# Seven block products also in the first feed-forward product of a two-layer decoder, and V and rotation tables in the shared tile pool

## The chip, the cores and the metric

The kernel runs on one NeuronCore of one Trainium2 chip. The metric is the device time of one execution in microseconds (us); less is better. The engines are PE (matmul, with PEld for its weight loads), DVE (VectorE), ACT (ScalarE), POOL (GpSimd) and SP (SyncE, which issues most DMAs).

## The reference, cut to what matters

```python
D_MODEL, SEQ, DEPTH, N_META = 1024, 512, 2, 16
D_FF = 4 * D_MODEL
...
def squared_relu_mlp(h, w1, w2):
    return jnp.square(jax.nn.relu(h @ w1)) @ w2
...
    for l in range(DEPTH):
        mix = hybrid_mixer(h, w_in[l], mla_q_norm[l], mla_kv_norm[l], w_uq[l], w_ukv[l], w_out[l], pos, valid)
        h = layer_norm(DN_ALPHA * h + mix, ln1_g[l], ln1_b[l])
        h = layer_norm(DN_ALPHA * h + squared_relu_mlp(h, w_ff1[l], w_ff2[l]), ln2_g[l], ln2_b[l])
    return h[:, N_PAD + N_META:]
```

All data are float32. `hybrid_mixer` runs eight heads of stick-breaking attention, eight of latent attention (MLA) and four of retention on one projection of `h`, and one output product over all of them. The rotation tables are the cosines and sines of `apply_rope`. Layer 0 works on 528 tokens (512 and 16 meta tokens), layer 1 on the 512 that are returned.

## The kernel before, in words

**Layout.** Activations lie transposed: 128 features on the partitions, tokens along the columns, so `h` is 8 tiles (`KT`) of up to 528 columns. Each float32 operand is held as two parts of type fp32r, hi (a rounded copy) and lo (the rest); a product of two tiles is three matmuls, hi*hi, hi*lo and lo*hi. `wload` brings 512 columns of weights by a DMA from SP into a tile of pool R; `wsplit` makes hi by a copy on ACT and lo by a subtraction on DVE, both in pool W. Pool U holds 63 tiles of 528 columns for everything else, V has its own pool VC, and five rotation tables lie in constants for the whole run (`tables`, line 520). Eight PSUM banks hold the products; `PM` and `PA` are two streams of the same eight.

**Feed-forward part** (`layer`, from line 1366). D_FF is cut in four quarters `qd` of 8 tiles. `ff1(qd, mt, c0, c1)` makes one tile of relu(h@w1)^2: 24 matmuls (8 tiles of `h`, three each) for a group of columns. In layer 0 the groups are 256 and 272 columns, in layer 1 one of 512. For quarters 0 to 2 the second product is made by `strassen(qd, m)`: for each pair of output tiles the 2 by 2 block product (block rows are the two output tiles, block columns the halves of H = 264 or 256 tokens, the inner blocks tiles i and i+4 of the quarter) is made with seven block products, 12 matmuls of H columns each, in place of eight, in the form of Winograd. `strassen_weights` makes the sums of weights (two by a DMA that adds, issued by POOL, two on DVE), `strassen_inputs` the sums of activations. Quarter 3 is made by plain `ff2`. Between the first product of a quarter and its seven-product part stands tile 0 of the next quarter's `ff1`. `nf=4`: the last four tiles of quarter 3 are made in two halves of columns, so that the layer norm of the first half runs beside the second.

**Order.** A recorder notes every operation (they all carry the profile's line 416), and `schedule` plays them through with the costs in nanoseconds of `_cost`: each engine takes the operation that can start first, then the one of lower rank. Tiles of a pool are handed out in the order in which they were recorded, within its capacity (`fits`); an operation whose tile isn't free waits. The order that comes out is what the engines run.

Of the kernel before, what the change touches and what calls it, by code (L numbers as in the profile page):

```python
# [15 lines left out]
P = 128  # L16
D = 1024
KT = D // P
# [21 lines left out]
    pvo=(-0.2, 0.0), mix=(0.9, 0.0), wl=0.0, wd=0.0, nw=4, nf=4, head=3, wc=512, wa=512,  # L40
# [185 lines left out]
class Recorder:  # L226
# [51 lines left out]
    @staticmethod  # L278
    def _cost(op, ins, outs):
        psum = any(v.t.cls.name == "ps" for v in ins)  # L280
        n = int(np.prod(outs[0].shape[1:])) if outs else 1
        op.ldw = 0.0
        if op.eng == "tensor":
            if op.fn == "transpose":
                n = op.args[1].shape[0]
                op.cost, op.ldw = n * 2 / 2.4 + 2, op.args[1].shape[1] / 1.2
            else:
                lt = op.kw["lhsT"]
                op.cost = n / 2.4 * (4 if lt.dtype == F32 else 1) + 2.5
                op.ldw = lt.shape[1] / (2.4 if lt.dtype == BF16 else 1.2)  # L290
        elif "dma" in op.fn:
            op.cost = 60.0
        elif op.eng == "scalar":
            op.cost = (54 if psum else 94) + 0.833 * n + 93 * (len(ins) - 1) + 93 * (len(outs) - 1)
        elif op.eng == "vector":
            fast = not psum and op.fn in ("tensor_copy", "tensor_scalar", "memset")
            if op.fn in ("bn_stats", "reduce_max"):
                n = int(np.prod(ins[0].shape[1:]))
            op.cost = 62 + n * (0.53 if fast else 1.05) + 62 * sum(isinstance(op.kw.get(k), View) for k in ("scalar", "scalar1", "scalar2"))
        else:  # L300
            op.cost = 80 + n * (2.4 if op.fn in ("tensor_sub", "tensor_add") else 1.2)
# [126 lines left out]
class Builder:  # L428
    def __init__(self, ctx, tc, a):
# [93 lines left out]
    def tables(self):  # L523
# [8 lines left out]
        for n in ("tqe", "tqo", "tkr", "rc", "rs"):  # L532
            tt = self.const(n, [P, NT], F32)
            nc.sync.dma_start(tt, a[n])
            self.tab[n] = tt
# [24 lines left out]
    def strassen_weights(self, l, qd, m):  # L560


        nc, src = self.nc, self.a["wf2"][l, qd, m]
        a11, a12, a21, a22 = (src[:, i:i + 512] for i in range(0, 2048, 512))
        t = {}
        with nc.rank(nc.cur + PR['wd']):
            for name, first, more in (("a12", a12, ()), ("s1", a21, (a22,)), ("a11", a11, ()), ("s3", a21, (a11,)),
                                      ("a22", a22, ())):
                t[name] = self.R.tile([P, 512], F32)
                nc.sync.dma_start(t[name], first)  # L570
                for x in more:
                    nc.gpsimd.dma_start(t[name], x, accum_op=ALU.add)
        w = {}
        for name in ("a12", "a11", "s1", "s2", "s4", "s3", "a22"):
            if name in ("s2", "s4"):
                x, y = ("s1", "a11") if name == "s2" else ("s2", "a12")
                t[name] = self.R.tile([P, 512], F32)
                nc.vector.tensor_add(t[name], t[x], t[y])
            w[name] = self.wsplit(t[name])
        return w  # L580

    def strassen_inputs(self, x, e, eh, el):

        nc = self.nc
        a, b = x
        H = e.shape[1]
        t = self.unit()
        b11, b12, b21, b22 = a[:, :H], a[:, H:2 * H], b[:, :H], b[:, H:2 * H]
        t3, t4, t2, t1 = t[:, :H], t[:, H:2 * H], e, b12
# [3 lines left out]
        nc.vector.scalar_tensor_tensor(out=t4, in0=t2, scalar=-1.0, in1=b21, op0=ALU.mult, op1=ALU.subtract)  # L593
        d = {}
        for x, names in ((b, ("b21", "b22")), (a, ("b11", "t1")), (e, ("t2",)), (t, ("t3", "t4"))):
            n = H * len(names)
            hi, lo = (eh, el) if x is e else (self.unit(F32R)[:, :n], self.unit(F32R)[:, :n])
            self.split(hi, lo, x[:, :n], "a")
            for i, k in enumerate(names):
                d[k] = (hi[:, i * H:i * H + H], lo[:, i * H:i * H + H])  # L600
        return d

# [53 lines left out]
    def ln_back(self, xns, gset, h, c0, c1):  # L656
# [4 lines left out]
        for kt in range(KT):  # L661
# [4 lines left out]
            hf = self.unit()[:, :c1 - c0]  # L666
# [19 lines left out]
    def ln_group(self, r, gset, h, c0, c1, final):  # L686
# [15 lines left out]
        if not final:  # L702
            self.ln_back(xns, gset, h, c0, c1)


    def v_tokens(self, w, b0, rhs, heads):
# [9 lines left out]
        V = self.VC.tile([P, 5, heads, 2, P // heads], F32R)  # L716
# [5 lines left out]
        s0 = p0[:, :P].reshape(heads, P // heads)  # L722
        nc.scalar.copy(V[:, 0, :, 0, :], s0)
        nc.vector.tensor_sub(V[:, 0, :, 1, :], s0, f32(V[:, 0, :, 0, :]))
        s1 = pv.reshape(4, heads, P // heads)
        nc.scalar.copy(V[:, 1:5, :, 0, :], s1)
        nc.vector.tensor_sub(V[:, 1:5, :, 1, :], s1, f32(V[:, 1:5, :, 0, :]))
# [3 lines left out]
    def pv_pair(self, s, hd, V, regs, meta):  # L731
# [5 lines left out]
        for i, j in enumerate(order):  # L737
            v = V[:, j, hd].reshape(P)
# [259 lines left out]
    def ret_attn(self, l, hd, st, V, gate):  # L998
# [73 lines left out]
    def mla_c(self, l, h):  # L1072
# [45 lines left out]
        wkr = self.wload(self.a["win"][l, 29])  # L1118
        kt, kth, ktl = self.unit(), self.unit(F32R), self.unit(F32R)
        krh, krl = self.unit(F32R), self.unit(F32R)  # L1120
        for (c0, c1) in self.groups(True):
# [3 lines left out]
            nc.vector.tensor_mul(kt[:, c0:c1], ps[:, :n], self.tab["tkr"][:, c0:c1])  # L1125
# [8 lines left out]
    def mla_proj(self, l, p, cn, kr):  # L1134
# [19 lines left out]
        for hd in range(2):  # L1154
            tab = self.tab["tqe" if hd == 0 else "tqo"]
# [139 lines left out]
    def layer(self, l, h, first):  # L1295
# [20 lines left out]
        for hd in range(4):  # L1316
# [49 lines left out]
        r_mix, r = r, [None] * KT  # L1366
        nf = PR['nf']
        NQ = NT if full else NX
        H = NQ // 2
        us, ws3 = [[] for _ in range(4)], [{} for _ in range(4)]  # L1370
        raw = [{} for _ in range(4)]
        half = [None]

        def ff1(qd, mt, c0, c1):
            n = c1 - c0
            if mt not in ws3[qd]:
                ws3[qd][mt] = self.wload(self.a["wff1"][l, 8 * qd + mt])
                if qd == 3:
                    us[qd].append((self.unit(F32R), self.unit(F32R)))
                else:  # L1380
                    raw[qd][mt] = self.unit()
            ps = self.mmb()
            self.proj(ps[:, :n], ws3[qd][mt], 0, h, c0, c1)
            rl = self.unit()[:, :n]
            nc.scalar.activation(rl, ps[:, :n], AF.Relu)
            if qd == 3:
                nc.scalar.activation(rl, rl, AF.Square)
                self.split(us[qd][mt][0][:, c0:c1], us[qd][mt][1][:, c0:c1], rl, "a")
                return
            x = raw[qd][mt]  # L1390
            nc.scalar.activation(x[:, c0:c1], rl, AF.Square)
            if c1 == NQ and mt >= 4:
                i = mt - 4
                if i % 2 == 0:
                    half[0] = self.unit(F32R), self.unit(F32R)
                c = slice((i % 2) * H, (i % 2) * H + H)
                us[qd].append(self.strassen_inputs((raw[qd][i], x), self.unit()[:, :H], half[0][0][:, c], half[0][1][:, c]))

        def ff2(qd, mt, w, c0, c1):
            n = c1 - c0  # L1400
            ps = self.mmb()
            self.proj(ps[:, :n], w, 0, us[qd], c0, c1)
            self.accum(ps[:, :n], r[mt][:, c0:c1], None, c0, c1)

        def strassen(qd, m):
            w = self.strassen_weights(l, qd, m)
            if qd == 0:
                for mt in (2 * m, 2 * m + 1):
                    r[mt] = self.unit()
            X, Y, Z = (self.mmb()[:, :H] for _ in range(3))  # L1410
            touched = set()

            def prod(ps, wk, uk, first, last):
                wh, wl = w[wk]
                for i in range(4):
                    b = slice(i * P, i * P + P)
                    uh, ul = us[qd][i][uk]
                    self.mm(ps, wh[:, b], uh, first and i == 0, False)
                    self.mm(ps, wh[:, b], ul, False, False)
                    self.mm(ps, wl[:, b], uh, False, last and i == 3)  # L1420

            def add(ps, row, col, op=ALU.add):
                mt, c = 2 * m + row, slice(col * H, col * H + H)
                o = r[mt][:, c]
                if qd == 0 and (row, col) not in touched:
                    touched.add((row, col))
# [224 lines left out]
```

## Time and profile before

| | |
|---|---|
| median of 3 runs | 1570.37 us (1570.01 to 1570.98) |
| the profiled execution | 1570.71 us, span 1568.9 us |
| mean granted TensorE clock | 0.996 |
| PE, PEld busy | 1535.4 us (98%), 1448.0 us (92%) |
| DVE, ACT busy | 1169.5 us (75%), 880.4 us (56%) |

The span runs from the first to the last instruction; 1.8 us of the profiled execution lie outside it. Busy times are unions of the recorded intervals; a matmul's interval is longer than its share of the engine, since matmuls are pipelined and their ends modelled, so in what follows matmuls are counted per stretch of time.

### The profile page before, as it was taken

Reading aid. Unit: us, or ns where it says so; the run is one execution under the profiler, and the core shown is the slowest. Engines: PE = TensorE matmul, PEld = TensorE weight load, DVE = VectorE, ACT = ScalarE, POOL = GpSimd, SP = SyncE. Lnnn points to the kernel's source line nnn. Section 1 sums busy time; section 2 is a strip of 40 time slices with the busy share of each in tenths; the row PEclk is TensorE's granted clock in tenths of the full one; section 3 lists DMA queues with packets and bytes.
Section 4 is the critical chain, followed back from the end, with each engine's and each line's share of the span. In section 5 each row is a group of like instructions: output and inputs, shape, how many; then the busy total and the mean of one; then the engine's idle time right before and its main releaser. Section 6 shows DMA issues by size and latency. Waiting matters only on the chain.

```text
span 1568.9 us, 30040 instructions
## 1 busy us (share of the span) xinstructions
PE 1535.4 (98%) x11130; PEld 1448.0 (92%) x11130; DVE 1169.5 (75%) x2791; ACT 880.4 (56%) x1979; POOL 145.9 (9%) x249
## 2 busy tenths in 40 slices
PE   6999999999999999999999999999999999999996
PEld 6999999989999999999999999888889898989986
DVE  7778877899787868674467878779997786767635
ACT  5575744578566464645336666445884645555440
POOL 4112100100001000010002112001100010101000
PEclk9999999999999999999999999999999999999998
DMA  6423422322024636354214233423222354545422
GB/s 231 120 70 112 134 68 69 92 65 76 29 84 111 169 101 167 101 147 132 89 61 129 80 96 95 125 68 98 72 68 63 106 150 127 148 135 130 153 61 81
DMA packets 88978, 165.26 MB, mean 105 GB/s; under 512 B 12032, under 2 KB 13312, under 8 KB 88832
## 3 DMA queue, kind: packets, MB, share of 16 engines
q1 hardware_dynamic: 76800, 136.77, 28.2%
q0 software_dynamic: 12032, 26.59, 8.4%
q8 instruction: 87, 1.43, 0.4%
q14 instruction: 59, 0.48, 0.1%
HBM read 142.92 MB, written 2.10 MB: 92 GB/s over the span
## 4 chain that ended last, share of the span: by engine, by line
PE 92%; DVE 4%; ACT 2%; issue 1%; DMA 0%; SPq 0%; DVEq 0%; ACTq 0%; POOLq 0%
PE ps L416 92%; DVE u L416 2%; ACT u L416 2%; DVE t L416 2%; DVE w L416 0%; DMA r<-in_win 0%; SPq L416 0%; DMA u<-u 0%; ACT w L416 0%; ACT t L416 0%; DVE v L416 0%; DVEq L1646 0%; ACTq L416 0%; DVEq L416 0%; POOLq L416 0%
## 5 line engine op out<-in xcount | busy, mean ns | idle before, releaser
L416 PE MATMUL ps<-u,w 128*128 128x256 f32 (+3 forms) x9024 | 1312.6, 303 | 3.1 <-DVE u L416 2.0
L416 PEld LDWEIGHTS ps<-u,w 128*128 128x128 f32 x9024 | 1203.1, 189 | 63.2 <-DVE u L416 3.4
L416 ACT CAST w<-r 128x512 fp32r<-128x512 f32 (+1 forms) x520 | 315.4, 618 | 384.2 <-PE ps L416 352.4
L416 DVE TENSOR_TENSOR w<-r,w 128x512 fp32r<-128x512 f32 (+1 forms) x514 | 350.3, 688 | 179.2 <-ACT w L416 152.4
L416 DVE TENSOR_TENSOR u<-u,u 128x512 fp32r<-128x512 f32 (+11 forms) x467 | 247.1, 552 | 40.2 <-ACT u L416 37.5
L416 ACT ACTIVATE u<-ps 128x256 f32<-128x256 f32 (+7 forms) x237 | 114.1, 486 | 116.6 <-PE ps L416 106.9
L416 ACT CAST u<-u 128x512 fp32r<-128x512 f32 (+6 forms) x247 | 128.8, 540 | 45.9 <-DVE u L416 39.9
L416 DVE TENSOR_TENSOR u<-u,ps 128x256 f32<-128x256 f32 (+3 forms) x220 | 95.4, 436 | 65.0 <-PE ps L416 62.5
L416 DVE TENSOR_TENSOR u<-ps,u 128x16 fp32r<-128x16 f32 (+14 forms) x312 | 115.3, 400 | 21.8 <-ACT u L416 14.6
L416 ACT ACTIVATE u<-u 128x256 f32<-128x256 f32 (+5 forms) x245 | 124.0, 521 | 5.4 <-DVE u L416 1.3
L416 PE MATMUL ps<-ident,u 128*128 128x128 f32 x672 | 104.6, 279 | 15.6 <-DVE t L416 9.6
L416 POOL DMA_DIRECT2D u<-u x112 | 58.2, 525 | 520.8 <-ACT u L416 484.0
L416 PE MATMUL ps<-u,u 128*128 128x512 f32 (+4 forms) x528 | 103.4, 314 | 0.0
L416 PEld LDWEIGHTS ps<-ident,u 128*128 128x128 f32 x672 | 79.8, 142 | 23.8 <-DVE t L416 8.4
L416 POOL DMA_DIRECT2D r<-in_wf x48 | 42.1, 877 | 588.9 <-DVE w L416 255.8
L416 PE MATMUL ps<-u,v 128*128 128x400 f32 (+4 forms) x484 | 89.1, 301 | 2.0 <-DVE u L416 0.6
L416 PEld LDWEIGHTS ps<-u,u 128*128 128x128 f32 x528 | 79.8, 190 | 2.6
L416 PEld LDWEIGHTS ps<-u,v 128*128 128x128 f32 x484 | 72.1, 189 | 7.0 <-ACT u L416 2.5
L416 ACT COPY u<-ps 128x256 f32<-128x256 f32 (+5 forms) x108 | 43.9, 416 | 41.2 <-PE ps L416 39.9
L416 DVE SCALAR_TENSOR_TENSOR u<-ps,u 128x432 f32<-128x432 f32 (+7 forms) x73 | 41.4, 579 | 27.6 <-ACT u L416 24.9
L416 ACT CAST u<-ps 128x16 fp32r<-128x16 f32 (+7 forms) x188 | 49.9, 331 | 18.7 <-PE ps L416 13.3
L416 ACT ACTIVATE u<-ps,t 128x512 f32<-128x512 f32 (+4 forms) x86 | 48.1, 562 | 18.4 <-DVE t L416 16.1
(66 smaller groups left out, 758.1 us busy)
## 6 DMA issues: line engine op xcount, KB each, us to landing
r<-in_wff SPq DMA_DIRECT2D x160, 256.0 KB, 2.9
r<-in_win SPq DMA_DIRECT2D x120, 256.0 KB, 2.9
r<-in_wf SPq DMA_DIRECT2D x120, 256.0 KB, 3.1
r<-in_wout SPq DMA_DIRECT2D x48, 256.0 KB, 2.9
r<-in_wf POOLq DMA_DIRECT2D x48, 256.0 KB, 4.7
u<-u POOLq DMA_DIRECT2D x80, 132.0 KB, 3.6
u<-u SPq DMA_DIRECT2D x48, 66.0 KB, 2.7
u<-in_xm SPq DMA_DIRECT2D x10, 256.0 KB, 5.3
```

Source lines behind the costliest of these rows:

```text
L416: o.ins = getattr(getattr(nc, o.eng), o.fn)(*[r(x) for x in o.args], **{k: r(x) for k, x in o.kw.items()})
```

## The change

The first product gets pairs of tiles (i, i+4) by seven block products too: all pairs of quarters 1 to 3 and pair 3 of quarter 0 (`npl=3` pairs stay plain), 13 of 16. The sums of `h` are made once for each layer. Two of the four pairs of quarter 3's second product are made by seven block products, in place of none. One function `strassen` runs both. In `ff1_pair` the blocks of the output come out of PSUM one after the other, bank X is read after each of x1, x2, x3 and x4, and the squares and the second product's sums are made per block. The residual's start value is a float32 copy of `h` (`raw`) that the layer norm leaves, in place of hi and lo. V (three tiles in place of one of VC) and the rotation tables (loaded in each layer, where they are used) come from pool U, which has 75 tiles. The planner's costs are changed, and the tile of the next quarter between the two products is gone.

```diff
-    pvo=(-0.2, 0.0), mix=(0.9, 0.0), wl=0.0, wd=0.0, nw=4, nf=4, head=3, wc=512, wa=512,
+    pvo=(-0.2, 0.0), mix=(0.9, 0.0), wl=0.0, wd=0.0, nw=4, nf=4, npl=3, head=3, wc=512, wa=512,
...
-                op.cost = n / 2.4 * (4 if lt.dtype == F32 else 1) + 2.5
+                op.cost = 4 + 0.4445 * n
...
-            op.cost = (54 if psum else 94) + 0.833 * n + 93 * (len(ins) - 1) + 93 * (len(outs) - 1)
+            op.cost = (100 if psum else 125) + 0.833 * n + 100 * (len(ins) - 1) + 180 * (len(outs) - 1)
...
-            op.cost = 62 + n * (0.53 if fast else 1.05) + 62 * sum(isinstance(op.kw.get(k), View) for k in ("scalar", "scalar1", "scalar2"))
+            op.cost = 85 + n * (0.55 if fast else 1.04) + 55 * sum(isinstance(op.kw.get(k), View) for k in ("scalar", "scalar1", "scalar2"))
...
-        self.U = Pool(self.sb, "u", NT, 63).stream(63)
+        self.U = Pool(self.sb, "u", NT, 75).stream(75)
-        self.VC = Pool(self.sb, "v", 1280, 3).stream(3)
...
+    def table(self, n):
+        t = self.unit()
+        self.nc.sync.dma_start(t, self.a[n])
+        return t
...
+        load("s1", a21, a22)
+        load("a11", a11)
+        load("a12", a12)
+        w["s1"] = self.wsplit(t["s1"])
+        w["a11"] = self.wsplit(t["a11"])
+        add("s2", "s1", "a11")
+        load("s3", a21, a11)
+        add("s4", "s2", "a12")
+        w["s4"] = self.wsplit(t["s4"])
+        w["s2"] = self.wsplit(t["s2"])
+        load("a22", a22)
+        w["a12"] = self.wsplit(t["a12"])
+        w["s3"] = self.wsplit(t["s3"])
+        w["a22"] = self.wsplit(t["a22"])
...
+    def strassen(self, w, us, order, H, done):
+        X, Y, Z = (self.mmb()[:, :H] for _ in range(3))
+        prods = dict(y=(Y, "a12", "b21", True, True), x1=(X, "a11", "b11", True, False), z1=(Z, "s1", "t1", True, False),
+                     x2=(X, "s2", "t2", False, False), z2=(Z, "s4", "b22", False, True), x3=(X, "s3", "t3", False, False),
+                     x4=(X, "a22", "t4", False, True))
+        n = len(us)
+        for k in order:
+            ps, wk, uk, first, last = prods[k]
...
+                self.mm(ps, wh[:, b], uh, first and i == 0, False)
+                self.mm(ps, wh[:, b], ul, False, False)
+                self.mm(ps, wl[:, b], uh, False, last and i == n - 1)
+            if k in done:
+                done[k](X, Y, Z)
...
+        def ff1_pair(qd, i):
+            w = self.strassen_weights(self.a["wff1"][l, 8 * qd + i], self.a["wff1"][l, 8 * qd + i + 4])
...
+            def square(x, scale, src):
+                nc.scalar.activation(x, src, AF.Relu, scale=scale)
+                nc.scalar.activation(x, x, AF.Square)
...
+            def x1(X, Y, Z):
+                nc.vector.tensor_add(b11, X, b11)
+                square(b11, 1.0, b11)
+            def x2(X, Y, Z):
+                nc.vector.tensor_add(b12, X, b12)
+                square(b12, 1.0, b12)
+                sub(t1, b11, b12)
...
+                    parts(p, ("b11", "t1"))
+            def x3(X, Y, Z):
+                nc.vector.tensor_add(b22, X, z1)
+                square(b22, -1.0, b22)
+                sub(t3, b22, b12)
+                stt(out=t2, in0=t3, scalar=-1.0, in1=b11, op0=ALU.mult, op1=ALU.subtract)
+                parts(t2, ("t2",), *(x[:, o] for x in self.half[0]))
+                if qd < 3:
+                    parts(q, ("b22", "t3"))
+            def x4(X, Y, Z):
+                square(b21, -1.0, X)
+                stt(out=t4, in0=t2, scalar=-1.0, in1=b21, op0=ALU.mult, op1=ALU.subtract)
...
+            self.strassen(w, hs, ("z1", "y", "x1", "z2", "x2", "x3", "x4"), H, dict(
+                z1=lambda X, Y, Z: nc.scalar.copy(z1, Z), y=lambda X, Y, Z: nc.scalar.copy(b11, Y),
+                z2=lambda X, Y, Z: nc.scalar.copy(b12, Z), x1=x1, x2=x2, x3=x3, x4=x4))
...
+            self.strassen(w, us[qd], ("z1", "x1", "z2", "x2", "y", "x3", "x4"), H, dict(
...
-            if qd < 3:
-                for g in gl:
-                    ff1(qd + 1, 0, *g)
...
+        for i in range(npl, 4):
+            ff1_pair(0, i)
+        for m in range(4):
+            ff2_pair(0, m)
+        for qd in range(1, 4):
+            for i in range(4):
+                ff1_pair(qd, i)
+            for m in range(4 if qd < 3 else 4 - nf // 2):
+                ff2_pair(qd, m)
```

## Rows read from the trace of the kernel before

**Rows 1.** The page's part 1: busy us (share of the span) xinstructions.

```profile
PE 1535.4 (98%) x11130; PEld 1448.0 (92%) x11130; DVE 1169.5 (75%) x2791; ACT 880.4 (56%) x1979; POOL 145.9 (9%) x249
```

**Rows 2.** The page's part 4, the chain that ended last, by engine.

```profile
PE 92%; DVE 4%; ACT 2%; issue 1%; DMA 0%; SPq 0%; DVEq 0%; ACTq 0%; POOLq 0%
```

**Rows 3.** Who waited for whom, PE's waits: us in total, times, longest.

```profile
PE ps L416 <- DVE t L416: 10.2, 4, 8.4
PE ps L416 <- DVE u L416: 6.8, 8, 2.3
PE ps L416 <- ACT u L416: 3.8, 5, 1.4
```

**Rows 4.** Busy us (xinstructions) by stretch; then granted clock, DMA share, GB/s.

```profile
core 0: us, PE busy (x) PEld busy (x) DVE busy (x) ACT busy (x) POOL busy (x), PEclk, DMA share, GB/s
300.00:400.00 100.00, 95.82 (x717) 88.81 (x716) 91.21 (x316) 76.58 (x245) 11.24 (x32) 0.98 0.26 74
...
460.00:500.00 40.00, 40.00 (x329) 40.00 (x328) 28.14 (x55) 27.12 (x61) 3.57 (x4) 1.00 0.45 113
...
510.00:540.00 30.00, 30.00 (x248) 30.00 (x247) 27.39 (x58) 12.29 (x21) 2.62 (x3) 1.00 0.69 183
550.00:580.00 30.00, 30.00 (x249) 30.00 (x248) 19.05 (x36) 19.17 (x42) 2.63 (x3) 1.00 0.37 92
595.00:625.00 30.00, 30.00 (x249) 30.00 (x248) 24.28 (x46) 12.66 (x21) 3.50 (x4) 1.00 0.67 178
...
1080.00:1180.00 100.00, 98.64 (x607) 84.88 (x606) 92.34 (x293) 81.11 (x247) 6.60 (x17) 1.00 0.26 76
...
1310.00:1340.00 30.00, 30.00 (x131) 24.36 (x130) 18.82 (x35) 17.79 (x32) 2.62 (x3) 1.00 0.39 102
...
1352.00:1382.00 30.00, 30.00 (x257) 30.00 (x256) 25.39 (x47) 13.54 (x22) 3.50 (x4) 1.00 0.71 190
```

**Rows 5.** Timeline: start us, us of the merged run, engine, operation, count.

```profile
419.89 1.08 DVE L416 TENSOR_TENSOR u<-u,ps 128x256 f32<-128x256 f32 x3 [1.21 <-PE ps L416]
421.67 0.42 DVE L416 TENSOR_TENSOR u<-u,ps 128x256 f32<-128x256 f32 x1 [0.70 <-PE ps L416]
...
602.22 1.14 ACT L416 CAST w<-r 128x512 fp32r<-128x512 f32 x2 [0.83 <-PE ps L416]
...
605.60 1.29 DVE L416 TENSOR_TENSOR w<-r,w 128x512 fp32r<-128x512 f32 x2
```

**Rows 6.** Instruction groups by shape, 450 to 800 us: count | busy us, mean ns.

```profile
L416 DVE TENSOR_TENSOR w<-r,w 128x512 fp32r<-128x512 f32 x159 | 108.5, 690 | 71.2 <-ACT w L416 56.4 <-PE ps L416 8.6 <-issue 0.5
L416 ACT CAST w<-r 128x512 fp32r<-128x512 f32 x160 | 97.0, 620 | 131.5 <-PE ps L416 116.1 <-issue 6.6 <-DVE r L416 4.3
L416 DVE TENSOR_TENSOR u<-u,ps 128x264 f32<-128x264 f32 x68 | 28.9, 427 | 11.0 <-PE ps L416 10.8
L416 DVE TENSOR_TENSOR u<-u,u 128x528 fp32r<-128x528 f32 x36 | 25.3, 702 | 0.0
...
L416 DVE TENSOR_TENSOR r<-r,r 128x512 f32<-128x512 f32 x24 | 16.4, 685 | 0.1
L416 ACT ACTIVATE u<-u 128x272 f32<-128x272 f32 x32 | 13.8, 432 | 0.9
...
L416 ACT ACTIVATE u<-ps 128x272 f32<-128x272 f32 x32 | 12.6, 394 | 3.1 <-PE ps L416 3.0
```

**Rows 7.** DMA issues: count, KB each, median us from issue to landing.

```profile
r<-in_wf SPq DMA_DIRECT2D x120, 256.0 KB, 3.1
r<-in_wf POOLq DMA_DIRECT2D x48, 256.0 KB, 4.7
...
rc<-in_rc SPq DMA_DIRECT2D x1, 264.0 KB, 4.3
```

**Rows 8.** Waits of the queue on SP: us in total, times, longest.

```profile
SPq L416 <- DVE w L416: 969.4, 328, 17.1
```

More of the change, by code (lines that the diff above doesn't have):

```diff
@@ L558, in wsplit, with strassen_weights, load @@
         return hi, lo
-    def strassen_weights(self, l, qd, m):
-        nc, src = self.nc, self.a["wf2"][l, qd, m]
-        a11, a12, a21, a22 = (src[:, i:i + 512] for i in range(0, 2048, 512))
+    def strassen_weights(self, src1, src2):
+        nc = self.nc
+        a11, a12, a21, a22 = src1[:, 0:512], src1[:, 512:1024], src2[:, 0:512], src2[:, 512:1024]
         t = {}
[L566 to L569, printed above, removed]
+        def load(name, first, more=None):
+            t[name] = self.R.tile([P, 512], F32)
+            with nc.rank(nc.cur + PR['wd']):
@@ L570, in strassen_weights @@
                 nc.sync.dma_start(t[name], first)
-                for x in more:
-                    nc.gpsimd.dma_start(t[name], x, accum_op=ALU.add)
-        w = {}
[L574 to L579, printed above, removed]
+                if more is not None:
+                    nc.gpsimd.dma_start(t[name], more, accum_op=ALU.add)
@@ new lines, in add @@
+        def add(name, x, y):
+            t[name] = self.R.tile([P, 512], F32)
+            nc.vector.tensor_add(t[name], t[x], t[y])
+        w = {}
+        load("s1", a21, a22)
[9 more added lines that the diff above has]
+        load("a22", a22)
@@ L601, in strassen_inputs, with parts, run @@
-        return d
+    def parts(self, d, H):
+        def run(x, names, hi=None, lo=None):
+            n = H * len(names)
+            if hi is None:
+                hi, lo = self.unit(F32R)[:, :n], self.unit(F32R)[:, :n]
+            self.split(hi, lo, x[:, :n], "a")
+            for j, k in enumerate(names):
+                d[k] = (hi[:, j * H:j * H + H], lo[:, j * H:j * H + H])
+            return hi, lo
+        return run
+    def strassen_inputs(self, a, b, H, i):
+        t, e = self.unit(), self.unit()[:, :H]
+        if i % 2 == 0:
+            self.half = [(self.unit(F32R), self.unit(F32R))]
+        o = slice((i % 2) * H, (i % 2) * H + H)
+        self.strassen_sums(a, b, a[:, H:2 * H], e, t)
+        d = {}
+        parts = self.parts(d, H)
+        parts(a, ("b11", "t1"))
+        parts(e, ("t2",), *(x[:, o] for x in self.half[0]))
+        parts(b, ("b21", "b22"))
+        parts(t, ("t3", "t4"))
+        return d
@@ L715, in v_tokens @@
                 yield
-        V = self.VC.tile([P, 5, heads, 2, P // heads], F32R)
+        n = 2 * P
+        U = [self.unit(F32R) for _ in range(3)]
+        V = [U[0][:, :n].reshape(heads, 2, P // heads)]
+        for u in U[1:]:
+            V += [u[:, i * n:i * n + n].reshape(heads, 2, P // heads) for i in range(2)]
         p0 = self.mmb()
@@ L1372, in layer, with ff1 @@
-        half = [None]
-        def ff1(qd, mt, c0, c1):
+        us, xs, hs = [[] for _ in range(4)], {}, []
+        touched = set()
+        nf = PR['nf']
+        def ff1(mt, c0, c1):
             n = c1 - c0
[L1376 to L1381, printed above, removed]
+            if mt not in xs:
+                xs[mt] = self.wload(self.a["wff1"][l, mt]), self.unit()
+            w, x = xs[mt]
@@ L1382, in ff1 @@
             ps = self.mmb()
[L1383 removed]
+            self.proj(ps[:, :n], w, 0, h, c0, c1)
             rl = self.unit()[:, :n]
             nc.scalar.activation(rl, ps[:, :n], AF.Relu)
[L1386 to L1391 removed]
@@ L1400, in ff2 @@
+        def ff2(mt, w, c0, c1):
             n = c1 - c0
             ps = self.mmb()
[L1402 removed]
+            self.proj(ps[:, :n], w, 0, plain, c0, c1)
             self.accum(ps[:, :n], r[mt][:, c0:c1], None, c0, c1)
[L1405 to L1426, printed above, removed]
[L1427 to L1445 removed]
@@ new lines, in layer @@
+        for (hi, lo), x in sums:
+            self.split(hi, lo, x, "a")
+        for i in range(npl):
+            us[0].append(self.strassen_inputs(xs[i][1][:, :NQ], xs[i + 4][1][:, :NQ], H, i))
+        for i in range(npl, 4):
[3 more added lines that the diff above has]
+        for qd in range(1, 4):
+            for i in range(4):
+                ff1_pair(qd, i)
+            for m in range(4 if qd < 3 else 4 - nf // 2):
+                ff2_pair(qd, m)
@@ L1471, in layer @@
+        plain = [u["plain"][0] for u in us[3]] + [u["plain"][1] for u in us[3]]
         final = l == DEPTH - 1
-        ws = {mt: self.wload(self.a["wff2"][l, 0, mt]) for mt in range(8 - nf, 8)}
+        ws = {mt: self.wload(self.a["wff2"][l, 3, mt]) for mt in range(8 - nf, 8)}
         for i, g in enumerate(gs):
```

198 lines of the change are left out of this document (102 added, 96 removed).

## The prediction, as it was put on record before the run

> **What bounds the kernel now.** I read the page's busy shares first: PE is busy for 98% of the span, DVE for 75%, ACT for 56% [rows 1]. The chain that ended last says the same, 92% of it is PE [rows 2], and PE's own waits add up to 10.2 + 6.8 + 3.8 = 20.8 us, 8.4 of it in one wait for a tile t of statistics [rows 3]. A busy PE may still be a slow one, so next I counted matmuls per stretch. In the feed-forward part they follow one another without holes: 248 records touch 510:540, two of them lap in from the edges, so one of 264 columns takes 30/246 = 0.122 us; the plain stretch 550:580 gives the same, layer 1's 257 of 256 columns give 30/255 = 0.1176 us, and its 131 of 512 columns 30/129 = 0.2325 us [rows 4]. The reader should see two more things there. In the seven-product stretches DVE is at 27.39 of 30 us (91%, quarter 0) and 24.28 (81%), and PE keeps its full count beside it. And in the latent attention, where DVE shows 91.21 and 92.34 of 100 us and ACT 76.58 and 81.11, the matmul counts drop (717 small and large ones in 100 us): there DVE, ACT and PE hold each other up [rows 4]. So PE's count is what the feed-forward part costs, as long as DVE is not filled.
>
> **The change, part by part.**
>
> *Removed from PE.* A pair of tiles by eight block products is 96 matmuls of H columns, by seven 84. Per layer 13 pairs of the first product and 2 of the second change, 15 in all. Layer 0: 12 x 0.122 = 1.464 us a pair, 22.0 us. Layer 1: plain is 48 of 512 columns, 48 x 0.2325 = 11.16 us; seven products of 256 columns are 84 x 0.1176 = 9.88 us; 1.28 a pair, 19.2 us. Sum 41.2 us; that is the ceiling, since no operation is added to PE.
>
> *Added to DVE in a first-product pair.* Records of DVE overlap: a lone subtraction of 512 columns shows 690 ns [rows 6], but two in a row take 1.29 us, so the second costs 1.29 - 0.69 = 0.60; three of 256 columns take 1.08 us and a lone one 0.42, so (1.08 - 0.42)/2 = 0.33 each, and I take 0.34 for 264 and 0.62 for 528. On ACT two of 512 take 1.14 us, 0.52 each [rows 5]. A pair then needs on DVE 7 weight subtractions and 2 weight sums (9 x 0.60), 3 adds from PSUM and 4 sums (7 x 0.34), and the lo parts of 528, 528, 528 and 264 columns (3 x 0.62 + 0.34): 9.98 us, beside 84 x 0.122 = 10.25 us of PE. Plain it was 4 x 0.60 + 4 x 0.34 + 2.20 = 5.96. In layer 1 it is 9.84 beside 9.88. In quarter 3 one more short subtraction makes it 10.32. ACT: 7 x 0.52 for the weights, 3 copies and 8 squares or relus at about 0.3 to 0.43 [rows 6], 2.0 for the splits, some 9.4 us. So DVE goes from half full to 97 to 101% full, and ACT to about 90%.
>
> [...]
>
> *What that costs.* Below: nothing. Averaged over a quarter DVE needs 4 x 9.98 and, with 9 x 0.60 + 7 x 0.34 = 7.78 for each pair of the second product, 4 x 7.78, together 71.0 us in 8 x 10.25 = 82.0 (87%), and pool W holds one pair's weights (14 tiles) ahead; at 91% by the record, in 510:540, PE lost nothing [rows 4]. Above: each pair by itself, with DVE kept only 92% busy as in 1080:1180 [rows 4]. Layer 0: 9.98/0.92 = 10.85, 0.60 over PE, x13 = 7.8; layer 1: 9.84/0.92 = 10.70, 0.82 over, x13 = 10.7; quarter 3's extra 0.34/0.92 x 8 = 3.0; 21.5 us. I take 12, a bit over half: the stretch is nearer to the seven-product one in its kind of work, but at its demand no row shows PE undisturbed, and each of the eight passages from first to second product must drain DVE's chain (add, relu, square, subtraction, split) with no tile of the next quarter between.
>
> *Start of the part.* The sums of `h` are new: 4 x (4 x 0.34 + 0.62 + 2 x 0.34) = 10.6 us of DVE per layer, after the second half's layer norm. Of the nine tiles that stood before the first seven-product part, 329/48 = 6.9 were made after 460 us [rows 4]; with three tiles fewer, PE has four left there (4 x 48 x 0.122 = 23.4 us) and one new pair, 33.7 us; DVE has 8 x 0.60 for weights, 10.6, the inputs of three pairs 3 x 3.56 = 10.7, the pair's 9.98 and 5.4 for the next weights: 41.5. Above, 7.8 us a layer; below about 1, since five of those seven splits and the late inputs can come while PE is at the first products. Before, DVE had 28.14 of these 40 us filled [rows 4]. I take 2.5, for two layers 5.
>
> *Second product.* Residual from `raw`: one instruction for each block in place of two, 16 x 0.34 = 5.4 us of DVE less in quarter 0, hidden as now; nothing.
>
> *DMAs.* A new pair takes 5 loads by SP and 2 adding ones by POOL, in place of 4 and 0; adding ones go from 48 to 108, 4.7 us to landing, behind 3.1 for the load they add to [rows 7]. The DMA share stands at 0.69 in a seven-product stretch [rows 4] and a pair lasts 10 us, so I take nothing; a cover lost shows as POOL waiting and PE waiting for weights, about 2 us at a passage, which the 12 holds.
>
> *Tables and V.* Ten table loads in place of five, each 4.3 us to landing [rows 7], in SP's queue behind weight loads, which wait for tiles up to 17.1 us [rows 8]; behind a late one stands one DVE multiplication and the projection's bank. Below nothing, above 4.3 us a layer for one late table; I take nothing, since the pool hands tiles out ahead. V's copies in three pieces, not two, add 24 short pairs, 24 x (2 x 0.33 - 0.60) = 1.4 us on DVE; nothing.
>
> *Planner's costs.* A matmul of 264 columns is planned at 121 ns (112 before), as measured; a DVE subtraction of 512 at 617 (600) and an ACT copy at 551 (520), 3 to 6% over the rows [rows 5]. The mixer is put in another order; sign unknown, zero, and 5 us either way, a quarter of PE's 20.8 us of waits [rows 3].
>
> *Sum.* 1570.7 (the profiled execution, 0.3 over the median) - 41.2 + 12 + 5 = 1546.5; against the median 1546.
>
> **The rivals.**
>
> *DVE becomes the bound.* Both upper bounds: 1570.7 - 41.2 + 21.5 + 15.6 = 1566.6, with a late table in each layer 1575; around 1568. For it: 97 to 101% demand; the latent attention, where 92% goes with lost matmuls. Against it: the 87% over a quarter.
>
> *DVE's records do not overlap in the new mix.* Dependent instructions (sum on sum) follow one another without the gain of 0.69 - 0.60 = 0.09 us. If all paid the whole record [rows 6], a pair would need 9 x 0.690 + 7 x 0.427 + 3 x 0.702 + 0.427 = 11.7 us, 1.5 over PE, in layer 1 (0.69 and 0.42) 11.6, 1.75 over, x13 each = 42: 1570.7 - 41.2 + 42 + 5 = 1577. Against it: pairs in a row in rows 5 do overlap. [...]
>
> *Bank X is the bound* (slower). x2, x3 and x4 follow one another into one bank, and each must wait until DVE has read the last: a read of 0.43 us behind an instruction of 0.60 in DVE's queue, 1.0 each, two a pair. If PE has nothing to put between, 26 x 2.0 = 52 us: 1570.7 - 41.2 + 52 + 5 = 1586. It decides from (41.2 - 5)/26 = 1.39 us a pair. Behind x3 then stand x4 and the next pair's products; only the next pair's z1 and y can fill, if two triples of banks and its weights are free. For it: DVE's queue is full now. Against it: the second product ends with x3, x4 in the same way, and its stretches keep full count [rows 4].
>
> *All is hidden.* 1570.7 - 41.2, with 2 to 8 us for the starts: 1532 to 1538.
>
> That the products are not saved can't be: their number is fixed.
>
> **How the numbers follow.** Forecast, 1546 (1538 to 1560): 0.53. DVE the bound, 1560 to 1575: 0.19. No overlap: 0.02. Bank X: 0.10. All hidden: 0.16. The range 1532 to 1571 holds all of the first, nearly all of the last and most of the second, 0.83. A measurement tells about 0.2% (3 us): faster takes the first and last and 0.10 of the second, 0.79; within 0.2%, 0.07 of it; slower the rest, 0.14.
>
> **What would show it.** Layer 0 must lose 15 x 12 = 180 matmuls; in layer 1 15 x 48 = 720 of 512 columns become 15 x 84 = 1260 of 256. In the new first-product stretches DVE should show 93% or more, beside about 245 matmuls in 30 us; under 235, DVE is the bound, and the waits of PE name DVE u. Waits of PE before x3 and x4 inside the pairs, not at the ends of quarters, would be bank X. In quarter 0, where DVE has 41.5 us of work in 33.7 of PE, PE should wait a few us for hi and lo parts. Wrong would be a mixer that moves by more than 5 us, or new waits of PE for DMA r.

## The result and the profile after

The changed kernel takes 1547.31 us, the median of four runs (1544.35 to 1547.67), against 1570.19 (1569.96 to 1570.98) for the kernel before, run beside it: a ratio of 0.9851, 95% interval 0.9839 to 0.9862. The forecast was 1546, faster. The profiled execution took 1546.99 us, with a span of 1545.2.

The page's parts 1 and 4 of the changed kernel, which answer to [rows 1] and [rows 2]:

```profile
PE 1504.6 (97%) x11490; PEld 1443.6 (93%) x11490; DVE 1303.8 (84%) x3131; ACT 963.7 (62%) x2263; POOL 197.9 (13%) x309
...
PE 87%; DVE 9%; ACT 2%; issue 1%; DMA 0%; SPq 0%; DVEq 0%; ACTq 0%
```

PE has 360 records more, as it must: 180 fewer in layer 0, and in layer 1 1260 of 256 columns in place of 720 of 512. Its busy time falls by 30.8 us, while DVE's rises by 134.3 and ACT's by 83.3. DVE's share of the chain that ended last goes from 4 to 9%.

PE's waits (in total, times, longest), to be read against [rows 3]:

```profile
PE ps L414 <- DVE u L414: 10.9, 16, 2.0
PE ps L414 <- DVE t L414: 9.2, 2, 7.9
PE ps L414 <- ACT w L414: 5.2, 9, 1.5
PE ps L414 <- ACT u L414: 2.5, 5, 0.6
```

One kind of wait is new: PE waits for a weight tile w from ACT, nine times. No wait for a DMA is among them.

Busy time by stretch, with the columns of [rows 4]. The first row and the one of 1060:1160 are the latent attention; 545:575 and 1295:1325 lie in the new first-product stretches; the rest is quarter 0 and the passages from the first to the second product:

```profile
300.00:400.00 100.00, 96.57 (x731) 89.51 (x730) 92.05 (x322) 77.62 (x250) 11.24 (x32) 1.00 0.26 74
478.00:498.00 20.00, 16.88 (x134) 16.25 (x133) 19.61 (x41) 15.59 (x36) 2.86 (x4) 1.00 0.55 148
500.00:530.00 30.00, 30.00 (x249) 30.00 (x248) 26.96 (x53) 12.60 (x22) 5.25 (x6) 1.00 0.74 186
545.00:575.00 30.00, 30.00 (x249) 30.00 (x248) 29.08 (x57) 26.45 (x64) 4.38 (x5) 1.00 0.69 171
575.00:587.00 12.00, 10.45 (x68) 9.72 (x68) 10.22 (x21) 6.74 (x16) 1.75 (x2) 0.86 0.40 112
660.00:670.00 10.00, 8.45 (x67) 8.02 (x66) 9.59 (x20) 6.81 (x15) 0.88 (x1) 1.00 0.55 140
1060.00:1160.00 100.00, 99.74 (x610) 85.69 (x610) 91.04 (x290) 80.16 (x245) 7.79 (x21) 1.00 0.26 74
1230.00:1250.00 20.00, 17.43 (x129) 16.62 (x128) 18.04 (x38) 14.10 (x31) 3.47 (x4) 0.91 0.61 160
1295.00:1325.00 30.00, 30.00 (x257) 30.00 (x256) 28.95 (x59) 27.23 (x67) 4.38 (x5) 1.00 0.69 174
1324.00:1331.00 7.00, 6.34 (x48) 5.60 (x47) 7.00 (x16) 4.84 (x12) 1.75 (x2) 1.00 0.67 171
```

Inside the new stretches DVE is busy for 97% (29.08 and 28.95 of 30 us) and ACT for 88 to 91%, and PE keeps its full count: 249 records of 264 columns and 257 of 256, as in [rows 4]. What PE loses lies at the passages. In 575:587, 98 matmuls of 0.122 us would fit and 68 stand there: 30 x 0.122 = 3.7 us gone. In 660:670 it is 15 of 82 (1.8 us), in 478:498, quarter 0, 30 of 164 (3.7 us).

The whole account, from the starts of all matmuls (what each start comes later than the count of its width allows): the products save 40.1 us; PE loses 20.9 in the two feed-forward parts, 9.0 of it in quarter 0 (3.9 and 5.1) and 11.9 at the later passages (4.0 and 2.1 at the first two of layer 0, 0.6 to 2.1 at the others); the rest comes out 4.5 us shorter. 1570.7 - 40.1 + 20.9 - 4.5 = 1547.0.

The passage at 575:587 by itself, PE's timeline (start, us, count, and in brackets its idle time before and who ended it):

```profile
575.80 3.68 PE L414 MATMUL ps<-u,w 128*128 128x264 f32 x29
580.00 0.51 PE L414 MATMUL ps<-u,w 128*128 128x264 f32 x2 [0.52 <-ACT w L414]
581.14 0.51 PE L414 MATMUL ps<-u,w 128*128 128x264 f32 x2 [0.64 <-ACT w L414]
582.05 3.29 PE L414 MATMUL ps<-u,w 128*128 128x264 f32 x13 [0.40 <-ACT u L414]
```

and ACT's:

```profile
579.33 0.61 ACT L414 CAST w<-r 128x512 fp32r<-128x512 f32 x1
579.84 0.41 ACT L414 CAST u<-u 128x264 fp32r<-128x264 f32 x1
580.16 0.42 ACT L414 ACTIVATE u<-u 128x264 f32<-128x264 f32 x1
580.48 0.60 ACT L414 CAST w<-r 128x512 fp32r<-128x512 f32 x1
```

PE runs two matmuls and stops, twice: each time 0.05 to 0.06 us after ACT has made a hi copy of a weight (579.33 + 0.61 = 579.94, PE at 580.00). Matched with the order in which the program issues them, these are the first products, z1 and x1, of the *second* pair of the second product. The two tiles of pool w that ACT writes for them had been released only at 578.62, by x4 of the last first-product pair, and at 578.99, by z1 of the first pair of the second product; ACT, which has other work in its queue without a gap there, came to them 0.7 and 1.5 us later. So what is late is a weight tile, because pool w's 14 tiles are one pair's seven hi and seven lo parts. The third pause, 0.40 us before 582.05, is another: there PE waits for an input, the last pair's, which has come through DVE and ACT. After these pauses the granted clock falls to 0.50 for 3.4 us:

```profile
582.30:585.70 3.40, 3.40 (x16) 3.38 (x16) 2.08 (x4) 0.22 (x1) 0.31 (x1) 0.50 0.51 172
```

so that the mean of the row 575:587 is 0.86. Some 1.7 of this passage's 4.0 us are that (an estimate: half of 3.40 us; by the count, 16 records stand there where 28 would fit, 12 x 0.122 = 1.5).

### The profile page after: what moved, and what is told of

Same layout as the page of the kernel before. It is cut to its first block, busy times and chain, and to the rows that moved or that the text cites. A ratio compares the mean times of both kernels' runs of the same rounds, so it can differ in the third digit from the quotient of the medians.

```text
span 1545.2 us, 31629 instructions
## 1 busy us (share of the span) xinstructions
PE 1504.6 (97%) x11490; PEld 1443.6 (93%) x11490; DVE 1303.8 (84%) x3131; ACT 963.7 (62%) x2263; POOL 197.9 (13%) x309
## 4 chain that ended last, share of the span: by engine, by line
PE 87%; DVE 9%; ACT 2%; issue 1%; DMA 0%; SPq 0%; DVEq 0%; ACTq 0%
PE ps L414 87%; DVE u L414 6%; ACT u L414 2%; DVE t L414 2%; DVE w L414 1%; DMA u<-in_xm 0%; SPq L414 0%; DVE r L414 0%; ACT w L414 0%; DVEq L1738 0%; ACT t L414 0%; DVEq L414 0%; ACTq L414 0%
## 5 line engine op out<-in xcount | busy, mean ns | idle before, releaser
L414 ACT CAST w<-r 128x512 fp32r<-128x512 f32 x610 | 364.5, 617 | 293.0 <-PE ps L414 249.2
L414 DVE TENSOR_TENSOR w<-r,w 128x512 fp32r<-128x512 f32 x604 | 404.8, 686 | 59.2 <-ACT w L414 42.9
L414 DVE TENSOR_TENSOR u<-u,u 128x512 fp32r<-128x512 f32 (+10 forms) x541 | 283.3, 548 | 10.8 <-ACT u L414 8.9
L414 DVE TENSOR_TENSOR u<-ps,u 128x256 fp32r<-128x256 f32 (+11 forms) x518 | 198.0, 409 | 48.3 <-ACT u L414 28.8
L414 PE MATMUL ps<-u,u 128*128 128x272 f32 (+5 forms) x1012 | 183.8, 307 | 1.7 <-ACT u L414 0.9
L414 POOL DMA_DIRECT2D r<-in_wff x108 | 94.8, 881 | 652.0 <-DVE u L414 331.4
L414 ACT CAST u<-u 128x512 fp32r<-128x512 f32 (+7 forms) x287 | 149.8, 540 | 39.9 <-DVE u L414 34.7
L414 ACT ACTIVATE u<-u 128x256 f32<-128x256 f32 (+5 forms) x349 | 161.7, 475 | 15.3 <-DVE u L414 12.3
L414 PEld LDWEIGHTS ps<-u,u 128*128 128x128 f32 (+1 forms) x1012 | 150.2, 190 | 8.6 <-ACT u L414 1.4
L414 ACT ACTIVATE u<-ps 128x512 f32<-128x512 f32 (+9 forms) x185 | 88.6, 484 | 89.8 <-PE ps L414 78.6
L414 DVE TENSOR_TENSOR r<-r,r 128x512 f32<-128x512 f32 x108 | 74.0, 685 | 2.3 <-DMA r<-in_wff 2.1
```

Of the source, the lines that this page charges most:

```text
L414: o.ins = getattr(getattr(nc, o.eng), o.fn)(*[r(x) for x in o.args], **{k: r(x) for k, x in o.kw.items()})
```

## The experiments

Each ran in five rounds beside the kernel before, whose median was 1570.2 to 1570.5 throughout; so the medians can be set beside the 1547.31 of the changed kernel ("after" below), and the ratios beside its 0.9839 to 0.9862. e4 to e13 are told in the order of the questions, not of their numbers.

**e1_npl4: all four pairs of quarter 0 plain, not three.**

```diff
-... nf=4, npl=3, head=3 ...
+... nf=4, npl=4, head=3 ...
```

> Quarter 0's last pair is made plain too (npl=4, 12 of 16 pairs by seven products). Both layers lose one pair's gain, 1.46 + 1.28 = 2.7 us. Theory (DVE is overfilled at the start of the part: sums of h, inputs and a new pair's weights in one stretch, which costs PE about 9 us of waits at 480 to 500 and 1230 to 1250 us of the changed kernel's trace): most of those waits go, 1547 + 2.7 - 7 = about 1543, DVE-released waits of PE in quarter 0 under 1 us a layer. Rival (the waits belong to every passage from first to second product, since no tile of the next quarter stands between): they stay, 1549 to 1550.

Measured: 1541.51 us, ratio 0.9817 (0.9802 to 0.9831), 5.8 below after, though the pair that is plain again in each layer gives up 1.46 and 1.28 us. Quarter 0 in it:

```profile
480.00:500.00 20.00, 19.83 (x160) 19.38 (x159) 19.37 (x41) 14.20 (x32) 1.75 (x2) 1.00 0.30 75
```

160 records in 20 us, nearly the full 164, as the theory had it. The one seven-product pair of quarter 0 costs more than it saves, with 14 tiles in pool w: its weights, its inputs and the sums of `h` come in the same stretch.

**e2_adjacent: z2 ahead of x1, so that all products into bank X follow one another.**

```diff
-("z1", "y", "x1", "z2", "x2", "x3", "x4")
+("z1", "y", "z2", "x1", "x2", "x3", "x4")
```

> Order of the seven products in a first-product pair z1, y, z2, x1, x2, x3, x4 in place of z1, y, x1, z2, x2, x3, x4, so that a third read of bank X (after x1) stands between two products into it with no product of the pair between. Theory (the planner puts the next pair's products between, and DVE's and ACT's full queues at the passages are the cost): within 4 us of 1547. Rival (bank X is the bound): one more exposed wait of 0.7 to 1.0 us in each of 26 pairs, 1565 to 1573.

Measured: 1549.10 us, 0.9862 (0.9848 to 0.9877). The intervals overlap; the medians differ by 1.8 us, where one more wait of 0.7 to 1.0 us in each of 26 pairs would have been 18 or more. So bank X's order is not what the lost time hangs on.

**e3_pool_lo: one of a pair's lo subtractions on POOL.**

```diff
-        w["a22"] = self.wsplit(t["a22"])
+        w["a22"] = self.wsplit(t["a22"], eng)   # eng = nc.gpsimd in ff1_pair
```

> In each first-product pair one of the seven weight subtractions (a22, the last one used) goes from DVE to POOL, where one takes 1.43 us. Theory (DVE is the engine that is full in the first-product stretches): 26 x 0.60 = 15.6 us of DVE less there, PE's waits of some 21 us at the passages shrink by a third or more, 1538 to 1543. Rival 1 (the passages cost what the chain add, relu, square, sum, split lasts, or ACT is as full as DVE): 1546 to 1549. Rival 2 (POOL delivers a22 too late, behind its adding DMAs): PE waits before x4, over 1550.

Measured: 1549.18 us, 0.9865 (0.985 to 0.988): no gain. DVE has 26 instructions fewer (3105), and yet its busy time is 1304.9 us, 1.1 more than after's. The groups by shape in 545:575, first of after, with count, busy time, mean ns:

```profile
L414 DVE TENSOR_TENSOR u<-u,u 128x528 fp32r<-128x528 f32 x9 | 6.3, 701 | 0.4 <-ACT u L414 0.4
...
L414 DVE TENSOR_TENSOR u<-u,u 128x264 f32<-128x264 f32 x5 | 2.1, 426 | 0.0
```

and of e3:

```profile
L414 DVE TENSOR_TENSOR u<-u,u 128x528 fp32r<-128x528 f32 x9 | 7.4, 820 | 0.0
L414 POOL TENSOR_TENSOR w<-r,w 128x512 fp32r<-128x512 f32 x3 | 5.4, 1816 | 21.3 <-ACT w L414 21.3
L414 DVE TENSOR_TENSOR u<-u,u 128x264 f32<-128x264 f32 x5 | 4.0, 805 | 0.2 <-ACT u L414 0.2
```

The three subtractions on POOL take 3 x 0.60 = 1.8 us from DVE and put 5 x (805 - 426) + 9 x (820 - 701) ns = 3.0 us back on it, on instructions that did not change. So this run did not relieve DVE, and says nothing on what DVE's load costs; its theory (1538 to 1543) was not put to the test. The next three runs do change that load.

**e6_dve_more: the same lo subtraction done twice on DVE.**

```diff
             (eng or nc.vector).tensor_sub(lo, raw, f32(hi))
+            if more:    # a22 of ff1_pair
+                nc.vector.tensor_sub(lo, raw, f32(hi))
```

> In each first-product pair the weight subtraction of a22 is done twice on DVE, 26 x 0.60 = 15.6 us more of DVE. Theory (DVE is full there, 97 to 101% before): nearly all of it comes out at the end, 1555 to 1563. Rival (DVE is not the limit, the chain's length or ACT is): 1546 to 1551.

Measured: 1549.65 us (1546.77 to 1553.95), 0.9863 (0.9846 to 0.9879). DVE's busy time goes up by 11.1 us (1314.9), the median by 2.3, within what the intervals leave open. Its stretch 545:575, in the profiled execution (1553.95, its slowest):

```profile
545.00:575.00 30.00, 29.72 (x244) 29.51 (x244) 29.01 (x57) 26.15 (x62) 5.25 (x6) 1.00 0.68 160
```

Five records fewer than after (249): with one more subtraction a pair, PE begins to be held up inside the stretch too. The theory, by which nearly all of the added work comes out at the end, did not hold (1555 to 1563); the rival's range did.

**e8_dve_squares: three of a pair's relu-and-square pairs as one instruction on DVE, off ACT.**

```diff
-                nc.scalar.activation(x, src, AF.Relu, scale=scale)
-                nc.scalar.activation(x, x, AF.Square)
+                if src is not x:
+                    nc.scalar.activation(x, src, AF.Relu, scale=scale)
+                    nc.scalar.activation(x, x, AF.Square)
+                    return
+                stt(out=x, in0=x, scalar=0.0, in1=x, op0=ALU.max if scale > 0 else ALU.min, op1=ALU.mult)
```

> Three of the four squared relus of a first-product pair become one DVE instruction each, max(x,0)*x, in place of two on ACT: ACT does about 2.0 us less for a pair, DVE 1.0 more, and the chain after x1, x2, x3 is shorter by an instruction and two changes of engine. Theory A (ACT's queue, in which weights and squares stand behind one another, and the chain's length make the waits at the passages): 1538 to 1544. Theory B (DVE is what is full): 26 x 1.0 = 27 us more of it, 1555 to 1570.

Measured: 1562.57 us, 0.995 (0.9938 to 0.9963), 15.3 over after, with 24.8 us more on DVE (1328.6) and 47.7 less on ACT (916.0). Its stretches:

```profile
545.00:575.00 30.00, 29.64 (x241) 29.23 (x240) 28.95 (x61) 20.96 (x46) 5.25 (x6) 1.00 0.63 147
1300.00:1330.00 30.00, 28.26 (x230) 28.06 (x229) 29.53 (x63) 20.46 (x45) 5.02 (x6) 0.96 0.67 156
```

PE is held up inside the stretches: 241 and 230 records where 249 and 257 stood, and its waits for DVE u go from 10.9 to 20.5 us:

```profile
PE ps L414 <- DVE u L414: 20.5, 25, 2.0
```

Here DVE holds PE up, as theory B had it (1555 to 1570). ACT is busy for only 20.5 to 21 of 30 us now, and that does not help; what less work on ACT would bring with DVE's left as it was, no run shows.

**e9_dve_less: the lo parts of s3 and a22 of each first-product pair are left out (set to zero by POOL), so the output lacks their share.**

```diff
-            (eng or nc.vector).tensor_sub(lo, raw, f32(hi))
+            if less:    # s3 and a22 of ff1_pair
+                nc.gpsimd.memset(f32(lo), 0.0)
+            else:
+                (eng or nc.vector).tensor_sub(lo, raw, f32(hi))
```

> Left out: the lo parts of weights s3 and a22 in first-product pairs are set to zero by POOL, which reads nothing for it, in place of two DVE subtractions; PE's matmuls stay. 26 x 1.2 = 31 us less of DVE. Theory B (DVE is full in the first-product stretches): the passages' waits shrink by more than half, 1532 to 1539. Theory A or C (ACT's queue, or pool W's tiles): 1543 to 1548.

Measured: 1538.70 us, 0.9799 (0.9786 to 0.9813): 8.6 below after for 25.6 us of DVE's busy time (1278.2). The passage in it:

```profile
575.00:587.00 12.00, 10.78 (x87) 10.36 (x86) 11.13 (x24) 7.34 (x16) 1.75 (x2) 1.00 0.62 145
```

87 of 98: without two of the nine weight operations in each pair the first passage still loses 11 x 0.122 = 1.3 us. Less on DVE helps, by a third of what is taken off; it does not clear the passages. The time lies in theory B's range, at its end, but what that theory says of the waits does not hold: PE's losses in the two feed-forward parts, counted as above, shrink by about a third and not by more than half, and its wait for ACT's w stays nearly what it was, 4.7 us after 5.2.

**e10_w18: four tiles more in pool w, taken from pool u.**

```diff
-        self.U = Pool(self.sb, "u", NT, 75).stream(75)
-        self.W = Pool(self.sb, "w", 512, 14).stream(14)
+        self.U = Pool(self.sb, "u", NT, 71).stream(71)
+        self.W = Pool(self.sb, "w", 512, 18).stream(18)
```

> Pool W gets 18 tiles and pool U 71 in place of 14 and 75 (the same bytes): weights of a pair and two parts of the next. Theory C (at a passage PE has only the next pair's products to put between, and their weights wait for a tile of W until the pair before has used it): waits released by ACT w at the passages go, 1540 to 1544. Theory A or B: within 2 us of 1547, or slower where U is now too small.

Measured: 1525.03 us (1523.11 to 1526.70), 0.9709 (0.9696 to 0.9722): 22.3 below after, with DVE's busy time the same (1303.1). It beats both kernels, and lies 15 us below what theory C expected. All its PE waits:

```profile
PE ps L414 <- DVE t L414: 9.6, 2, 8.4
PE ps L414 <- DVE u L414: 7.1, 10, 1.5
PE ps L414 <- ACT u L414: 2.3, 3, 1.4
```

and its stretches, with quarter 0 first and last and two passages between:

```profile
478.00:498.00 20.00, 19.90 (x162) 19.57 (x161) 19.59 (x40) 16.00 (x37) 3.49 (x4) 1.00 0.60 148
...
572.00:584.00 12.00, 12.00 (x101) 12.00 (x100) 11.39 (x25) 10.10 (x24) 1.75 (x2) 1.00 0.54 128
650.00:665.00 15.00, 15.00 (x126) 15.00 (x125) 14.50 (x31) 13.14 (x31) 1.75 (x2) 1.00 0.62 144
1220.00:1240.00 20.00, 19.83 (x164) 19.29 (x163) 19.72 (x41) 15.37 (x33) 3.46 (x4) 1.00 0.78 179
```

The wait for ACT's w is gone, the first passage is full (101 records, the 98 that fit and those that lap in from the edges) at full clock, and PE's losses in the feed-forward parts, counted as above, fall from 20.9 to 2.6 us. DVE is as full as before: 19.59 of 20 us in quarter 0, 95% at the passage. ACT has as much to do (960.4 us in all, after 963.7). Four tiles are two weights, as many as came late in the timeline above. The planner knows the pool's size, so the order of the instructions moves with it; the run shows the two together.

**e11_before_w18: the same in the kernel before** (w 14 to 18, u 63 to 59).

```diff
-        self.U = Pool(self.sb, "u", NT, 63).stream(63)
-        self.W = Pool(self.sb, "w", 512, 14).stream(14)
+        self.U = Pool(self.sb, "u", NT, 59).stream(59)
+        self.W = Pool(self.sb, "w", 512, 18).stream(18)
```

> The kernel before with 18 tiles in W and 59 in U. Theory (W is short only where two seven-product parts follow one another; before, plain tiles of the next quarter stand between and PE has no waits there): within 4 us of 1570. Rival (more weights ahead help the whole kernel, the 22 us of the same edit after the change have nothing to do with the passages): 1550 or less.

Measured: 1565.87 us, 0.9974 (0.9963 to 0.9984): 4.3 us, just over the 4 of the theory. So of e10's 22.3 some 4 would have been there without the change, if the two add up, and 18 answer to what the change brought, close to the 20.9 - 2.6 = 18.3 counted in the feed-forward parts.

**e12_w18_npl4 and e13_w18_npl2: e10 with four and with two plain pairs in quarter 0, so none and two by seven products.**

```diff
-... nf=4, npl=3, head=3 ...
+... nf=4, npl=4, head=3 ...   # e13: npl=2
```

> 18 tiles in W, and quarter 0's last pair plain (npl=4). Theory (with W large enough no wait is left at the start, so the pair made plain only loses its saved matmuls): 1525 + 2.7 = 1527 to 1529, the sign opposite to the same edit with 14 tiles, which gave 5.8 us. Rival (the start is short of DVE whatever W holds): 1519 to 1523.

> 18 tiles in W, and 14 of 16 pairs by seven products (npl=2). If matmuls alone decide: 1525 - 2.7 = 1522 to 1523. If DVE, which has the sums of h, two pairs' inputs and two new pairs at the start, is now overfilled there: waits of PE in quarter 0, 1526 to 1532.

Measured: e12 1525.73 us, 0.9719 (0.9706 to 0.9733), between its two ranges and not to be told from e10; with 14 tiles the same step gave 5.8 us. e13 1532.67 us, 0.9762 (0.9749 to 0.9775), 7.6 over e10 and just over its second range. What is new among its PE waits, and its stretch in quarter 0 of layer 0:

```profile
PE ps L414 <- DVE w L414: 5.1, 3, 3.3
...
468.00:480.00 12.00, 9.69 (x70) 8.63 (x70) 11.79 (x25) 8.08 (x20) 0.00 (x0) 1.00 0.15 52
```

The lo part of a weight, made by DVE, comes too late, with DVE busy for 11.79 of 12 us. So with 18 tiles one seven-product pair in quarter 0 costs about what its 2.7 us of saved matmuls bring, and with two DVE is the limit there.

**e4_old_costs and e5_before_new_costs: the planner's costs alone.** e4 is the changed kernel with the old costs, e5 the kernel before with the new ones.

```diff
-                op.cost = 4 + 0.4445 * n
+                op.cost = n / 2.4 * (4 if lt.dtype == F32 else 1) + 2.5
...
-            op.cost = 85 + n * (0.55 if fast else 1.04) + 55 * sum(...)
+            op.cost = 62 + n * (0.53 if fast else 1.05) + 62 * sum(...)
```

> The changed kernel planned with the planner's costs of before. Theory (the costs only reorder; the mixer's gain of some 5 us, 4.3 in layer 0 up to the layer norm, comes from them): the mixer loses that again and the passages are planned on too fast a PE, 1550 to 1558. Rival (the pool and tables gave it, the costs nothing): within 3 us of 1547.

> The kernel before, planned with the new costs alone. Theory (the costs pay where DVE and ACT are full and PE has to be ordered around them, so in the mixer they give the 2 to 3 us by which the old costs are slower in the changed kernel's mixer, and nothing in the old feed-forward part, which has no waits): 1565 to 1569. Rival (the 12 us that the old costs lose in the changed kernel are a property of the costs): 1556 to 1561.

Measured: e4 1559.38 us, 0.9929 (0.9917 to 0.9942), 12.1 over after; e5 1570.42, 1.0 (0.9991 to 1.0009). PE's waits in e4:

```profile
PE ps L416 <- ACT w L416: 13.1, 12, 1.8
PE ps L416 <- DVE u L416: 10.2, 19, 2.0
```

The wait for ACT's w is 13.1 us where after has 5.2. The new costs are worth nothing in the kernel before and 12 us in the changed one, both outside the ranges that were expected. Most of it is waits of PE (37.1 us in all, against 28.0), above all for weights. By the count of starts the feed-forward parts lose some 8.5 us more than in after, 5.8 of them in quarter 0 and the rest at the later passages. Which of the costs does it was not tried.

## Why the prediction came out

**The products: right.** 40.1 us saved, 41.2 put down; the count of records moved by the 360 that the change gives.

**The new stretches: the load was right, and PE kept its count.** DVE was to show 93% or more beside about 245 matmuls in 30 us; it shows 97% beside 249, and in layer 1 96.5% beside 257. This settles two rivals. If DVE's records did not overlap, a pair would need more of DVE than of PE, and PE could not have kept its count. They do overlap in the new mix: in quarter 0 a subtraction of 512 columns by itself takes 0.69 us (484.82), and at 486.05 three in a row take 1.89 us, 0.60 for each after the first. Bank X would have shown waits before x3 and x4 inside the pairs; there are none in 545:575, and e2, which crowds that bank more, costs about 2 us. Only in quarter 0, where DVE is at 98% in 478:498, does a wait of that kind stand, before x2 of its one pair. In layer 0 x1 ended at 483.89, and DVE came to read the bank 4 us later:

```profile
487.85 0.43 DVE L414 TENSOR_TENSOR u<-ps,u 128x264 f32<-128x264 f32 x1
...
488.33 8.22 PE L414 MATMUL ps<-u,w 128*128 128x264 f32 x65 [1.24 <-DVE u L414]
```

In layer 1 it is 2.0 us, at 1237.57.

"DVE the bound" was not the case, but it was near: e8's 24.8 us more on DVE brought 15.3, and its time, 1562.57, is inside that rival's 1560 to 1575. "All is hidden", 1532 to 1538, was not the case either; with four more tiles in pool w (e10) it nearly is.

**The 12 us: the size right (11.9), the place right, the cause wrong in the main.** The prediction laid it on DVE, whose chain must drain at each passage, and named pool w, one pair ahead, as the cover. The chain does drain there, but it is the cover that falls short. With four more tiles in pool w, the same work on DVE and ACT and the same fill, the passages cost next to nothing (e10); with a fifth less weight work on DVE and 14 tiles, the first passage still loses time (e9). The step that failed is "pool W holds one pair's weights (14 tiles) ahead": one pair ahead means that the weights of the next can be written only as the products of this one, and the last before it, release theirs, and ACT then has them behind other work (0.7 and 1.5 us at 575:587). DVE's load makes this worse, at no even price: 25.6 us off it gave 8.6 back (0.34 for each), 11.1 on it cost about 2 (unclear), 24.8 on it, with 47.7 off ACT, 15.3 (0.62 for each). That the number came out at 12 is in part luck, since it was chosen between 0 and 21.5.

**The start: mis-sized.** 5 us put down for both layers, 9.0 measured, within the bounds of 1 and 7.8 a layer. The trace names the same inputs that were counted (ACT's hi copy of the first weights of the second product, DVE's add in x1 and a sum behind z1); e1 gets the time back. e10 gets nearly all of it back too, with the pair kept, so here as well the pool was part of it, which the prediction's sum of DVE's work did not see.

**The rest: in bounds.** 4.5 us less in the mixers and between, where 0 with 5 either way stood; nearly all of it (4.4) lies ahead of layer 0's feed-forward part, whose long run of matmuls starts at 452.55 and not at 456.92. Its start in the kernel before, in after and in e4:

```profile
456.92 1.33 PE L416 MATMUL ps<-u,w 128*128 128x256 f32 x9
...
452.55 1.69 PE L414 MATMUL ps<-u,w 128*128 128x256 f32 x12
...
455.00 2.27 PE L416 MATMUL ps<-u,w 128*128 128x256 f32 x16
```

With the old costs (e4) the changed kernel keeps 1.9 of these 4.4 us, so the new costs bring the other 2.5 there; by themselves, in the kernel before, they bring nothing (e5). What else of the change does it was not tried, and stays open. The two errors, 4 us too little at the start and 4.5 too much here, cancel.

**Put at nothing, and found so:** the tables (each landing in 2.8 to 6.6 us, with no wait of PE for a DMA) and the adding loads, now 108 at 4.8 us, where 4.7 stood [rows 7]:

```profile
r<-in_wff POOLq DMA_DIRECT2D x108, 256.0 KB, 4.8
...
u<-in_rs SPq DMA_DIRECT2D x2, 264.0 KB, 6.6
```

V's pieces, put at nothing too, were not measured by themselves.

## What to carry to other kernels

When a change fills an engine beside the bound one, look for what it loses not in the steady stretch, where 97% cost nothing here, but at the passages, and ask there how many steps ahead the buffers reach: four tiles of weights brought 18 us here, close to half of what the saved matmuls did. A cover of exactly one step was not enough where the next step's work changed its kind. And when a kernel gets fuller, measure the costs of its planner again: the kernel before didn't feel the difference, the changed one would have paid 12 us.

## What was not expected of the hardware

In e3, DVE's sums of two tiles of pool u took longer where they met POOL's subtraction: in 545:575 those of 264 columns take 805 ns in the mean where the changed kernel has 426, and those of 528 columns 820 where it has 701. In e3's timeline, one of POOL's three subtractions and the sum of 528 columns that meets it, then one that meets none:

```profile
566.68 1.73 POOL L414 TENSOR_TENSOR w<-r,w 128x512 fp32r<-128x512 f32 x1 [6.33 <-ACT w L414]
```

```profile
567.17 1.81 DVE L414 TENSOR_TENSOR u<-u,u 128x528 fp32r<-128x528 f32 x1
...
574.25 0.69 DVE L414 TENSOR_TENSOR u<-u,u 128x528 fp32r<-128x528 f32 x1
```

1.81 us where one that meets none takes 0.69, and the longer part of it lies beside POOL's 1.73. POOL's three take 1.82 us in the mean there, where such a subtraction took 1.43 in after. In e9, where POOL fills weight tiles by a memset, which has no tile to read, the means of DVE's sums in 545:575 stay at 706 and 427 ns, as in after (701 and 426), beside four memsets of 529 ns. Moving a subtraction to POOL saved 0.60 us a time on DVE in e3 and cost it 1.0.
